# Queries and keys turned unsplit, two fp32 transposes in place of four fp32r ones, and split into high and low parts after the turn

## The chip, the cores and the metric

One core of a Trainium2 chip runs the whole program in one launch. The metric is device time in microseconds (us) of one execution. Engines are named as in the profile: PE is TensorE, DVE is VectorE, ACT is ScalarE, POOL is GpSimd, SP is the queue that issues most DMAs.

## What is computed

Two layers of a gated block over 528 tokens (16 meta tokens and 512 others) of width 1024. Each layer projects the normalised rows with one wide weight, and from the projection come attention queries (8 heads of 64), one key and one value head, index queries (8 heads of 64), one index key, a pooled branch and gates. The index scores choose 128 keys for each query, and attention runs over those.

```python
def hybrid_layer(x, norm_g, w_in, qn_g, kn_g, ...):
    h = rms_norm(x, norm_g)
    proj = jnp.einsum('btd,de->bte', h, w_in)
    q, k, v, gate_a, u_b, gate_b, q_idx, k_idx, w_idx, merge = jnp.split(proj, ...)
    q = apply_rope(rms_norm(q.reshape(B, T, 8, 64), qn_g), cos_h, sin_h)
    k = apply_rope(rms_norm(k, kn_g), cos, sin)
    q_idx = apply_rope(q_idx.reshape(B, T, 8, 64), cos_h, sin_h)
    k_idx = apply_rope(k_idx, cos, sin)
    attn = indexer_sparse_attention(q, k, v, q_idx, k_idx, w_idx, k_top)
    ...
# in the attention, for a block of queries
s = jnp.einsum('bqhd,bkd->bqhk', q_idx, k_idx)
score = jnp.einsum('bqhk,bqh->bqk', jax.nn.relu(s), w_idx * idx_scale)
_, sel = lax.top_k(score, k_top)
logits = jnp.einsum('bqhd,bqkd->bqhk', q, k[sel]) * attn_scale
```

## The kernel before, in words

**Precision by parts.** Most products run in fp32r, a shortened form of fp32. To keep accuracy, an operand is split into a high part (the value rounded to fp32r by an ACT copy) and a low part (the value less its high part, a DVE subtraction). A dense product is then three matmuls: high by high, low by high, high by low. A head of 64 numbers has room for both of its parts side by side: 64 partitions of high and 64 of low make one operand of 128 partitions. The key operand holds its high part in both halves (`KK[:, 0]`) and its low part in both halves (`KK[:, 1]`), so two matmuls give all four products of a head. `KI` is the same for the index key.

**Tokens and tiles.** `TOK` (line 26) cuts the tokens into a tile of 16 (t = 0, the meta tokens) and four of 128. Queries and keys come out of PE with tokens on the partitions, and have to be turned, so that the 64 numbers of a head lie on the partitions.

**What happens to a key tile** (`kv_post`, line 604). DVE multiplies the key (`g` = 0) and the index key (`g` = 1) by the rotation tables into `t1` and `t2`, POOL adds the two (line 633). In `second` DVE scales the key by its inverse norm, and ACT writes the high part twice into `ks` (line 640). In `third` DVE writes the low part twice. In `trans` PE turns the four blocks of `ks`, 128x128 fp32r each, and ACT copies the turned blocks into `KK` and `KI` (lines 650 and 651).

**What happens to a query tile** (`q_post`, line 656). A tile holds four heads. DVE makes `t1` and `t2`, POOL adds them (line 677), `second` writes the high parts into `qs` (ACT, line 686), `third` the low parts (DVE), `trans` turns four blocks of 128x128 fp32r (high and low of a head beside each other) and ACT copies 128x512 numbers into `qi` (index queries) or `qq` (queries) at line 697. There are 16 tiles of index queries and 16 of queries over both layers, 8 key tiles of 128 tokens and 2 of 16. The queries of the 16 meta tokens go through `q_post` with t = 0.

**What sets the order.** PE and DVE run in the order of the program text. ACT, POOL and SP are ordered by a scheduler. The text is paced by groups: `group_done` (line 367) ends a group of some 24 matmuls, and runs what `later(fn, n)` put off by n groups, then one piece of weight preparation, then pieces of the top-k selection (`sel`) as far as a budget of modelled PE and DVE times allows. `half_done` (line 361) is called twice in a group and issues index products or attention steps from `fill`. An index query's products are put into `fill` six groups after its projection (`FI`). PSUM tiles of turned blocks come from the ring `bank("a")`, four banks.

**Weights.** Each chunk of 256 columns is split as well. Some have their low part from ACT and a POOL DMA, others from DVE: the weight chunk of the second half of the index queries is split by two DVE subtractions of 128x1024 early in each layer, and the first matmuls that read its low part stand in the first group of that chunk, 16 matmuls after the group's begin.

**PE's transposes** name the turned tile and the unit matrix as operands: `a<-identr,qs` and `a<-identr,ks` are the fp32r ones, `a<-consts,lt` are transposes of unsplit fp32 tiles in the attention (line 821), where `consts` holds the fp32 unit matrix.

Of the kernel before, what the change touches and what calls it, by code (L numbers as in the profile page):

```python
# [91 lines left out]
def tile_block(ctx: ExitStack, tc: tile.TileContext, x, meta, w_in, pool_w, w_a, w_b, w_out, rows, hgain, c_tab, out):  # L92
# [10 lines left out]
    def f(ap):  # L103
        return ap.bitcast(F32)
# [3 lines left out]
    def bank(tag, dt=F32):  # L108
        return psum.tile([128, 512], dt, tag=tag, name=tag, bufs=BANKS[tag])
# [246 lines left out]
    credit = [0.0]  # L356

# [3 lines left out]
    def half_done():  # L361
        credit[0] += rate[0] / 2
        n = int(credit[0])
        credit[0] -= n
        pump(n)
# [24 lines left out]
    def flush():  # L390
        while pend:
            pend.popleft()[1]()
# [211 lines left out]
    def kv_post(l, t, ps):  # L604
# [9 lines left out]
        v1 = t1[:m, :128].rearrange("p (g d) -> p g d", g=2)  # L614
        for g, (C, S) in enumerate(((Cg, Sg), (ctab, stab))):
            dve.tensor_tensor(v1[:, g], p2[:, g], C[:m, t], op=OP.mult)
            dve.tensor_tensor(t2[:m, 64 * g:64 * g + 64].rearrange("p (a d) -> p a d", a=2),
                              p2[:, g].rearrange("p (a d) -> p a d", a=2)[:, ::-1, :],
                              S[:m, t].rearrange("p (a d) -> p a d", a=2), op=OP.mult)
# [13 lines left out]
        gp.tensor_tensor(t1[:m, :128], t1[:m, :128], t2[:m, :128], op=OP.add)  # L633
        ks = tmp.tile([128, 4, 128], F32R, tag="P", name="ks", bufs=PB)
        k4 = ks[:m].rearrange("p (g a) (b d) -> p g a b d", g=2, b=2)
        b1 = v1[:, :, None, :].to_broadcast([m, 2, 2, 64])

        def second():
            dve.tensor_scalar(t1[:m, :64], t1[:m, :64], rk[:m], None, op0=OP.mult)
            act.copy(k4[:, :, 0], b1)  # L640

        def third():
            dve.tensor_sub(k4[:, :, 1], b1, f(k4[:, :, 0]))

        def trans():
            tp = bank("a", F32R)
            for j in range(4):
                pe.transpose(tp[:, j * 128:j * 128 + m], ks[:m, j, :], identr[:m, :m])
            t4 = f(tp).rearrange("p (g j c) -> p g j c", g=2, j=2)
            act.copy(KK[:, :, s:s + m], t4[:, 0, :, :m])  # L650
            act.copy(KI[0][:, :, s:s + m], t4[:, 1, :, :m])
        later(second, 1)
        later(third, 2)
        later(trans, 4)

    def q_post(t, ps, normed, dst, g=0):
# [21 lines left out]
        if normed:  # L678
            qs = tmp.tile([128, 544], F32R, tag="L", name="qs", bufs=LB)[:, :512].rearrange("p (h c) -> p h c", h=4)
        else:  # L680
            qs = tmp.tile([128, 4, 128], F32R, tag="P", name="qs", bufs=PB)

        def second():
            if normed and t == 0:
                dve.tensor_tensor(v1, v1, rq[:m, :, None].to_broadcast([m, 4, 64]), op=OP.mult)
            act.copy(qs[:m, :, 0:64], v1)
            if normed and t:
                norms()
# [10 lines left out]
        later(third, QN if normed else QI)  # L699
        later(trans, QN + 1 + l if normed else QI + 1)  # L700
# [3 lines left out]
    def index_steps(i, g, qS):  # L704
        n = NK[i]
        for hh in range(4):
            h = 4 * g + hh
            r = tmp.tile([128, 544], F32, tag="L", name="r", bufs=LB)
            for o, w in KPARTS[i]:
                ps = bank("a")  # L710
                pe.matmul(ps[:, :w], qS[:, hh, :], KI[0][:, 0, o:o + w], start=True, stop=False)
                pe.matmul(ps[:, :w], qS[:, hh, :], KI[0][:, 1, o:o + w], start=False, stop=True)
                e = min(w, n - o)
                act.activation(r[:, n - 1::-1] if i == 0 else r[:, o:o + e], ps[:, :e], AF.Relu,  # L714
                               scale=wab[:, i, h:h + 1])
# [41 lines left out]
    def attention(ensure, later_rate, on):  # L757
        st, pvs, pms, turned = {}, {}, {}, []

        def logits(u):  # L760
# [7 lines left out]
            for hh in range(2):  # L768
                h = 2 * j + hh
                qS = QS[i, h // 4][:, h % 4, :]  # L770
# [811 lines left out]
```

## Time and profile before

| | |
|---|---|
| median of 3 runs | 738.46 us (737.41 to 738.52) |
| span of the profiled execution | 735.6 us, 2.9 us below the median of the runs |
| PE busy | 730.1 us (99%), 5949 matmuls |
| DVE busy | 586.2 us (80%) |
| ACT busy | 482.1 us (66%) |
| POOL busy | 254.2 us (35%) |
| granted TensorE clock | 0.999 |

The span runs from the first to the last instruction of the program. A row of the groups names the line, engine, operation, tiles (out<-in), partitions and shape, then the busy time, the mean of one and the idle time before. Matmuls overlap one another, so the mean duration of one is longer than what it takes of PE's time. What it takes is read from the starts of rows in the timeline: the time from the start of one row to the start of the next.

### The profile page before, as it was taken

How to read it: one execution, taken by the hardware profiler on the slowest of the kernel's cores; microseconds unless marked ns; L12 is line 12 of the kernel's file. 1: busy time of each engine (PE TensorE's matmuls, PEld its weight loads, DVE VectorE, ACT ScalarE, POOL GpSimd, SP SyncE). 2: the span in 40 equal slices, each digit the busy share in tenths (PEclk: the TensorE clock that was granted, in tenths of full speed). 3: DMA queues.
4: the chain of work that ended last, by engine and by line, in shares of the span. 5: the costliest groups of instructions: out<-in, count | busy, mean ns of one | idle time of the engine just before them, and what ended most of it. 6: DMA issues, size and time to landing. Idle time of an engine off the chain costs nothing.

```text
span 735.6 us, 16083 instructions
## 1 busy us (share of the span) xinstructions
PE 730.1 (99%) x5949; PEld 706.0 (96%) x5949; DVE 586.2 (80%) x1478; ACT 482.1 (66%) x1099; POOL 254.2 (35%) x336
## 2 busy tenths in 40 slices
PE   9999999999999999999999999999999999999998
PEld 8999998999999999999999989998899999999997
DVE  6966999998997775894348668999989978768874
ACT  6779735757788886543245796357588977775643
POOL 3751174731222211163247411757131231106300
PEclk9999999999999999999999999999999999999999
DMA  8767765964655434643523778659564654438832
GB/s 268 233 172 165 167 145 115 229 149 99 141 119 122 94 84 105 192 141 118 143 89 87 171 175 199 157 116 205 126 156 103 144 115 90 113 107 268 202 88 71
DMA packets 103566, 106.41 MB, mean 145 GB/s; under 512 B 5008, under 2 KB 83632, under 8 KB 103488
## 3 DMA queue, kind: packets, MB, share of 16 engines
q1 hardware_dynamic: 91888, 74.89, 34.5%
q0 software_dynamic: 11520, 30.41, 23.1%
q8 instruction: 46, 0.75, 0.4%
q14 instruction: 32, 0.26, 0.1%
q10 hardware_dynamic: 80, 0.08, 0.0%
HBM read 66.41 MB, written 8.55 MB: 102 GB/s over the span
## 4 chain that ended last, share of the span: by engine, by line
PE 99%; DVE 0%; issue 0%; ACT 0%; DVEq 0%
PE d L63 80%; PE a L63 13%; PE v L63 5%; DVE ot L63 0%; DVE w L63 0%; ACT w L269 0%; ACT osum L1121 0%; DVE idle L63 0%; DVE nf L63 0%; DVE ta L63 0%; DVEq L63 0%; DVE ones L63 0%; ACT p L1021 0%; DVE ss L63 0%; DVE mhalf L63 0%
## 5 line engine op out<-in xcount | busy, mean ns | idle before, releaser
L63 PE MATMUL d<-hhi,w 128*128 128x256 f32 (+3 forms) x1392 | 278.4, 291 | 0.0
L63 PEld LDWEIGHTS d<-hhi,w 128*128 128x128 f32 x1392 | 222.2, 188 | 3.0 <-issue 0.6
L63 PE MATMUL d<-hlo,w 128*128 128x256 f32 (+3 forms) x696 | 189.8, 289 | 0.0
L63 DVE TENSOR_TENSOR w<-raw,w 128x512 fp32r<-128x512 f32 (+1 forms) x156 | 121.5, 785 | 14.0 <-ACT w L269 13.2
L63 PEld LDWEIGHTS d<-hlo,w 128*128 128x128 f32 x696 | 131.3, 189 | 1.4 <-issue 0.2
L63 PE MATMUL d<-hsum,w 128*128 128x264 f32 (+1 forms) x720 | 95.5, 285 | 0.0
L63 PEld LDWEIGHTS d<-hsum,w 128*128 128x128 f32 x720 | 89.6, 188 | 0.7 <-issue 0.3
L63 PE MATMUL d<-w,hhi 128*128 128x256 f32 x576 | 86.1, 287 | 0.0
L269 ACT CAST w<-raw 128x512 fp32r<-128x512 f32 x132 | 79.0, 624 | 6.7 <-DMA raw<-s 5.9
L63 PEld LDWEIGHTS d<-w,hhi 128*128 128x128 f32 x576 | 74.7, 188 | 4.7 <-issue 3.5
L255 POOL DMA_DIRECT2D raw<-raw x22 | 19.9, 905 | 115.5 <-DMA raw<-in_w_in_dram 30.3
L63 DVE MATCH_REPLACE8 sc<-m,sc 128x400 f32<-128x400 f32 (+2 forms) x100 | 54.4, 547 | 0.0
L221 POOL DMA_DIRECT2D w<-raw x34 | 31.8, 951 | 64.1 <-ACT w L220 46.5
L63 DVE MAX8 m<-sc 128x8 f32<-128x400 f32 (+2 forms) x100 | 53.2, 556 | 0.9
L793 ACT ACTIVATE lt<-lt,mn,NR 128x144 f32<-128x144 f32 (+3 forms) x64 | 42.3, 663 | 12.8 <-DVE mn L63 12.8
L284 POOL DMA_DIRECT2D raw<-s x22 | 19.6, 891 | 87.9 <-DVE s L63 40.7
L63 DVE SCALAR_TENSOR_TENSOR sc<-r,wsg,sc 128x144 f32<-128x144 f32 (+3 forms) x56 | 32.4, 582 | 16.9 <-ACT r L714 14.7
L63 PE MATMUL d<-w,hlo 128*128 128x256 f32 x288 | 45.6, 281 | 0.0
L63 PE MATMUL d<-mhi,w 128*128 128x272 f32 (+2 forms) x192 | 45.5, 324 | 0.0
L808 POOL TENSOR_SCALAR pm<-lt,rs 128x16 f32<-128x16 f32 x48 | 26.3, 575 | 44.2 <-DVE rs L63 33.1
L677 POOL TENSOR_TENSOR t<-t,t 128x256 f32<-128x256 f32 (+1 forms) x34 | 32.3, 951 | 25.6 <-DVE t L63 25.2
L1427 POOL TENSOR_TENSOR hlo<-ta,hhi 128x256 fp32r<-128x256 f32 (+1 forms) x28 | 26.8, 965 | 41.6 <-PE d L63 29.4
(247 smaller groups left out, 1564.5 us busy)
## 6 DMA issues: line engine op xcount, KB each, us to landing
raw<-in_w_in_dram SPq DMA_DIRECT2D x88, 256.0 KB, 3.5
w<-raw POOLq DMA_DIRECT2D x34, 512.0 KB, 5.9
raw<-in_w_in_dram SPq DMA_DIRECT2D x32, 512.0 KB, 4.6
raw<-in_w_out_dram SPq DMA_DIRECT2D x12, 512.0 KB, 3.8
raw<-raw POOLq DMA_DIRECT2D x22, 256.0 KB, 4.2
raw<-s POOLq DMA_DIRECT2D x22, 256.0 KB, 3.7
kept<-res SPq DMA_DIRECT2D x16, 264.0 KB, 3.2
res<-kept SPq DMA_DIRECT2D x16, 264.0 KB, 6.2
```

The costliest lines, as they stand in the source:

```text
L63: return fn(*a, **k)
L221: gp.dma_start(t, raws[c][s], accum_op=OP.add)
L255: gp.dma_start(raws[c][0][:, 1], raws[c][0][:, 0], accum_op=OP.add)
L269: act.copy(t[:, 0], blk[src[n]])
L284: gp.dma_start(blk["a12"], blk["s2"], accum_op=OP.add)
L677: added[0] = gp.tensor_tensor(t1[:m, :256], t1[:m, :256], t2[:m, :256], op=OP.add).ins
L793: act.activation(L[hh][:, :n], L[hh][:, :n], AF.Exp, scale=NR[:, i, h:h + 1], bias=mn[:, hh:hh + 1], accum_out=sm[:, hh:hh + 1])
L808: (gp if j < 3 else dve).tensor_scalar(pms[i][:, 2 * j + hh, :], L[hh][:, 0:16], rs[:, hh:hh + 1], None, op0=OP.mult)
L1427: pool_end = gp.tensor_sub(hlo[:, j, a:a + n], d, f(hhi[:, j, a:a + n]))
```

## The change

- Unsplit fp32 tiles are turned. A query tile has two transposes of 128x128 fp32, each of two heads side by side, in place of four of fp32r. A key tile has two, one for the key and one for the index key, each of which lies twice beside itself, so that both halves of the partitions get it. For that the POOL sum writes 256 numbers per row (128 before), and DVE's scaling 128 (64 before).
- The parts are made after the turn. A turned block has one head on partitions 0 to 63 and another on 64 to 127, and the parts of a head have to end on both halves. For index queries ACT copies the turned block into `qf` in SBUF and writes each head's high part in its own half, and DVE subtracts into the other half (two subtractions of 64x256). For queries ACT writes the high parts of both heads of a block, DVE subtracts out of PSUM into the low parts (128x256), and one group later two ACT copies of 64x256 move a low part and a high part to the other half (`cross`). For keys ACT copies the turned block into `kf`, writes two high parts, and DVE subtracts twice.
- The heads of a tile then lie in another order, and `place(h)` gives the place of a head.
- A new queue, `soon`, holds DVE's subtractions until the second `half_done` after the transposes.
- An index query's transposes come one group earlier than before (there are no parts to wait for), those of a meta key tile one group earlier, those of the others in the same group as before. The meta tokens' queries are as before.

The diff, cut to its core:

```diff
     def half_done():
+        ticks[0] += 1
+        while soon_q and soon_q[0][0] <= ticks[0]:
+            soon_q.popleft()[1]()
         credit[0] += rate[0] / 2
...
+    def soon(fn):
+        soon_q.append((ticks[0] + 2, fn))
...
-        gp.tensor_tensor(t1[:m, :128], t1[:m, :128], t2[:m, :128], op=OP.add)
-        ks = tmp.tile([128, 4, 128], F32R, tag="P", name="ks", bufs=PB)
...
+        gp.tensor_tensor(t1[:m, :256].rearrange("p (g b d) -> p g b d", g=2, b=2),
+                         *(v2[:, o, :, None, :].to_broadcast([m, 2, 2, 64]) for o in range(2)), op=OP.add)
         def second():
-            dve.tensor_scalar(t1[:m, :64], t1[:m, :64], rk[:m], None, op0=OP.mult)
-            act.copy(k4[:, :, 0], b1)
-
-        def third():
-            dve.tensor_sub(k4[:, :, 1], b1, f(k4[:, :, 0]))
+            dve.tensor_scalar(t1[:m, :128], t1[:m, :128], rk[:m], None, op0=OP.mult)
 
         def trans():
-            tp = bank("a", F32R)
-            for j in range(4):
-                pe.transpose(tp[:, j * 128:j * 128 + m], ks[:m, j, :], identr[:m, :m])
-            t4 = f(tp).rearrange("p (g j c) -> p g j c", g=2, j=2)
-            act.copy(KK[:, :, s:s + m], t4[:, 0, :, :m])
-            act.copy(KI[0][:, :, s:s + m], t4[:, 1, :, :m])
+            tp = bank("a")
+            kf = tmp.tile([128, HB], F32, tag="tt", name="kf", bufs=6)
+            for g in range(2):
+                pe.transpose(tp[:, g * m:g * m + m], t1[:m, g * 128:g * 128 + 128], ident[:m, :m])
+            act.copy(kf[:, :2 * m], tp[:, :2 * m])
+            sides = [(K[:, 0, s:s + m], K[:, 1, s:s + m], kf[:, g * m:g * m + m]) for g, K in enumerate((KK, KI[0]))]
+            for hi, lo, k in sides:
+                act.copy(hi, k)
+
+            def low():
+                for hi, lo, k in sides:
+                    dve.tensor_sub(lo, k, f(hi))
+            soon(low)
         later(second, 1)
-        later(third, 2)
-        later(trans, 4)
+        later(trans, 4 if t else 3)
...
+        def paired():
+            tp = bank("a")
+            for b in range(2):
+                pe.transpose(tp[:, b * 128:(b + 1) * 128], t1[:, b * 128:(b + 1) * 128], ident)
+            own, other = slice(0, 64), slice(64, 128)
+            both = tp[:, :256].rearrange("p (b c) -> p b c", b=2)
+            if normed:
+                act.copy(dst[:, 0:2], both)
+
+                def cross():
+                    act.copy(dst[other, 0:2], f(dst[own, 2:4]))
+                    act.copy(dst[own, 2:4], both[other])
+                soon(lambda: dve.tensor_sub(dst[:, 2:4], both, f(dst[:, 0:2])))
+                later(cross, 1)
+                return
+            qf = tmp.tile([128, HB], F32, tag="tt", name="qf", bufs=6)[:, :256].rearrange("p (b c) -> p b c", b=2)
+            act.copy(qf, both)
+            heads = [(dst[own, 0:2], dst[other, 0:2], qf[own]), (dst[other, 2:4], dst[own, 2:4], qf[other])]
+            for hi, lo, q in heads:
+                act.copy(hi, q)
+
+            def low():
+                for hi, lo, q in heads:
+                    dve.tensor_sub(lo, q, f(hi))
+            soon(low)
+
+        if t:
+            if normed:
+                later(norms, 1)
+            later(paired, QN + 1 + l if normed else QI)
+            return
...
-        later(third, QN if normed else QI)
-        later(trans, QN + 1 + l if normed else QI + 1)
+        later(third, QN)
+        later(trans, QN + 1 + l)
+
+    def place(h):
+        return 2 * (h % 2) + h % 4 // 2
```

How the order moves on PE, in the first layer, from the end of the fourth key tile's projection on. Before (`ks` are the split keys, `qs` the split index queries, `VM` the meta values):

```order
L63 MATMUL a<-identr,ks 128x128 x8
L63 MATMUL a<-VM,consts 128x64
L63 MATMUL d<-w,hhi 128x256 x8
L63 MATMUL d<-w,hlo 128x256 x8
L63 MATMUL d<-w,hhi 128x256 x8
L63 MATMUL a<-identr,ks 128x16 x4
L63 MATMUL a<-identr,qs 128x128 x4
```

The same place of PE's order after the change (`t_292` and `t_308` are the key tiles 1 and 2, `t_407` the meta key tile, `t_415` and `t_447` the index queries of tiles 1 and 2):

```order
L63 MATMUL a<-consts,t_292 128x128 x2
L63 MATMUL a<-consts,t_308 128x128 x2
L63 MATMUL a<-VM,consts 128x64
L63 MATMUL a<-consts,t_407 128x16 x2
L63 MATMUL a<-consts,t_415 128x128 x2
L63 MATMUL d<-w,hhi 128x256 x8
L63 MATMUL d<-w,hlo 128x256 x8
L63 MATMUL d<-w,hhi 128x256 x8
L63 MATMUL a<-consts,t_447 128x128 x2
```

The eight transposes of two key tiles are four, the meta key and the first index query have moved ahead of a group of 24 matmuls, and the dense matmuls stand as they did.

DVE's order at the same point of the second layer, from the low part of the second index query to the second half of the weight chunk. Before (`t_5767` is key tile 4, `w<-raw,w` a half of the low part of the weights):

```order
L63 TENSOR_TENSOR qs<-t_5691,qs 128x4x64
L63 TENSOR_TENSOR ks<-t_5714,ks 128x2x128
L63 TENSOR_SCALAR t_5767<-t_5767,rk 128x64
L63 TENSOR_TENSOR t_5829<-d,consts 128x256
L63 TENSOR_TENSOR t_5830<-d,consts 128x256
L63 TENSOR_TENSOR w<-raw,w 128x1024
L63 TENSOR_TENSOR ks<-t_5767,ks 128x2x128
L63 TENSOR_TENSOR t_5871<-d,consts 128x256
L63 TENSOR_TENSOR t_5872<-d,consts 128x256
L63 TENSOR_TENSOR w<-raw,w 128x1024
```

DVE's order there after the change (`t_5744` is key tile 4; three subtractions of 128x128 into `KK` and `KI` stand ahead of the first row):

```order
L63 TENSOR_TENSOR KI<-kf,KI 128x128
L63 TENSOR_TENSOR KK<-kf,KK 128x16
L63 TENSOR_TENSOR KI<-kf,KI 128x16
L63 TENSOR_TENSOR qi<-qf,qi 64x256 x2
L63 TENSOR_SCALAR t_5744<-t_5744,rk 128x128
L63 TENSOR_TENSOR t_5804<-d,consts 128x256
L63 TENSOR_TENSOR t_5805<-d,consts 128x256
L63 TENSOR_TENSOR w<-raw,w 128x1024
L63 TENSOR_TENSOR qi<-qf,qi 64x256 x2
L63 TENSOR_TENSOR t_5839<-d,consts 128x256
L63 TENSOR_TENSOR t_5840<-d,consts 128x256
L63 TENSOR_TENSOR w<-raw,w 128x1024
```

The subtractions into `ks` and `qs` ahead of the transposes are gone, and subtractions into `KK`, `KI` and `qi`, which wait for PE's transposes and ACT's copies of them, stand ahead of both halves of the weights.

More of the change, by code (lines that the diff above doesn't have):

```diff
@@ L356, in tile_block @@
     credit = [0.0]
+    soon_q, ticks = deque(), [0]
+    def soon(fn):
+        soon_q.append((ticks[0] + 2, fn))
     sel = deque()
@@ L390, in flush @@
     def flush():
-        while pend:
-            pend.popleft()[1]()
+        while pend or soon_q:
+            (soon_q if soon_q else pend).popleft()[1]()
     def drain():
@@ L613, in kv_post @@
         t2 = tmp.tile([128, HB], F32, tag="tt", name="t2", bufs=6)
-        v1 = t1[:m, :128].rearrange("p (g d) -> p g d", g=2)
+        v2 = t2[:m, :256].rearrange("p (o g d) -> p o g d", o=2, g=2)
         for g, (C, S) in enumerate(((Cg, Sg), (ctab, stab))):
-            dve.tensor_tensor(v1[:, g], p2[:, g], C[:m, t], op=OP.mult)
-            dve.tensor_tensor(t2[:m, 64 * g:64 * g + 64].rearrange("p (a d) -> p a d", a=2),
+            dve.tensor_tensor(v2[:, 0, g], p2[:, g], C[:m, t], op=OP.mult)
+            dve.tensor_tensor(v2[:, 1, g].rearrange("p (a d) -> p a d", a=2),
                               p2[:, g].rearrange("p (a d) -> p a d", a=2)[:, ::-1, :],
@@ L677, in q_post @@
         added[0] = gp.tensor_tensor(t1[:m, :256], t1[:m, :256], t2[:m, :256], op=OP.add).ins
[L678 to L681, printed above, removed]
+        def paired():
[26 more added lines that the diff above has]
+            return
+        qs = tmp.tile([128, 544], F32R, tag="L", name="qs", bufs=LB)[:, :512].rearrange("p (h c) -> p h c", h=4)
         def second():
-            if normed and t == 0:
-                dve.tensor_tensor(v1, v1, rq[:m, :, None].to_broadcast([m, 4, 64]), op=OP.mult)
+            dve.tensor_tensor(v1, v1, rq[:m, :, None].to_broadcast([m, 4, 64]), op=OP.mult)
             act.copy(qs[:m, :, 0:64], v1)
-            if normed and t:
-                norms()
         def third():
@@ L710, in index_steps @@
                 ps = bank("a")
-                pe.matmul(ps[:, :w], qS[:, hh, :], KI[0][:, 0, o:o + w], start=True, stop=False)
-                pe.matmul(ps[:, :w], qS[:, hh, :], KI[0][:, 1, o:o + w], start=False, stop=True)
+                pe.matmul(ps[:, :w], qS[:, place(hh), :], KI[0][:, 0, o:o + w], start=True, stop=False)
+                pe.matmul(ps[:, :w], qS[:, place(hh), :], KI[0][:, 1, o:o + w], start=False, stop=True)
                 e = min(w, n - o)
@@ L769, in logits @@
                 h = 2 * j + hh
-                qS = QS[i, h // 4][:, h % 4, :]
+                qS = QS[i, h // 4][:, place(h), :]
                 for pi, (o, w) in enumerate(KPARTS[i]):
```

2 lines of the change are left out of this document (removed).

## The prediction

> **What bounds the kernel now.** I read the page first: the busy times, the chain that ended last and the granted clock.
>
> ```profile
> span 735.6 us, 16083 instructions
> PE 730.1 (99%) x5949; PEld 706.0 (96%) x5949; DVE 586.2 (80%) x1478; ACT 482.1 (66%) x1099; POOL 254.2 (35%) x336
> ...
> PEclk9999999999999999999999999999999999999999
> ...
> PE 99%; DVE 0%; issue 0%; ACT 0%; DVEq 0%
> ```
>
> PE is busy for 99% of the span at full clock, and 99% of the chain that ended last is PE itself. So what is taken off PE's stream shortens the program, and what is added to ACT, DVE or POOL costs nothing unless PE comes to wait for it. Next I asked what PE waits for. The list of waits has one entry for it:
>
> ```profile
> PE d L63 <- DVE ss L63: 1.5, 1, 1.5
> ```
>
> That one lies in the start, before any query. So there is no stall in the stages of the change that could hide a gain, and none whose going would add to it. A busy PE is not PE at its best, so the next question is what the transposes take of PE's time.
>
> **What the old transposes take.** The groups of PE, by shape, give the counts: index queries and queries, and keys.
>
> ```profile
> L63 PE MATMUL a<-identr,qs 128*128 128x128 f32 x128 | 14.9, 240 | 0.0
> L63 PE MATMUL a<-identr,ks 128*128 128x128 f32 x32 | 3.8, 252 | 0.0
> L63 PE MATMUL a<-consts,lt 128*128 128x128 f32 x160 | 22.7, 272 | 0.0
> ```
>
> 128 fp32r transposes are 32 query tiles of four, 32 are 8 key tiles of four. The third row is the nearest to the new ones: fp32 tiles turned with the fp32 unit matrix. The means are durations of overlapping matmuls and not what each takes, so I take that from starts. One whole group of PE's timeline in the first layer, from one turn of a query tile to the next:
>
> ```profile
> 50.32 0.46 PE L63 MATMUL a<-identr,qs 128*128 128x128 f32 x4
> 50.61 1.18 PE L63 MATMUL d<-w,hhi 128*128 128x256 f32 x8
> 51.63 1.11 PE L63 MATMUL d<-w,hlo 128*128 128x256 f32 x8
> 52.58 1.11 PE L63 MATMUL d<-w,hhi 128*128 128x256 f32 x8
> 53.52 0.45 PE L63 MATMUL a<-identr,qs 128*128 128x128 f32 x4
> ```
>
> From 50.32 to 53.52 are 3.20 us. Eight dense matmuls take 52.58 - 51.63 = 0.95, so 24 take 2.85, and the four transposes 0.35, each 0.088. The same for two fp32 transposes in the attention, with 12 dense matmuls between them and the last row:
>
> ```profile
> 180.88 0.38 PE L63 MATMUL a<-consts,lt 128*128 128x128 f32 x2
> 181.02 0.37 PE L63 MATMUL d<-hhi,w 128*128 128x264 f32 x1
> 181.22 0.28 PE L63 MATMUL d<-hlo,w 128*128 128x264 f32 x1
> ...
> 182.56 0.65 PE L63 MATMUL d<-hsum,w 128*128 128x264 f32 x4
> ```
>
> From 181.22 to 182.56 run 11 dense matmuls in 1.34, each 0.122. From 180.88 to 182.56 are 1.68, less 12 x 0.122 = 1.46: two fp32 transposes take 0.22, each 0.11. An fp32 transpose costs a quarter more than an fp32r one, and there are half as many.
>
> **PE's sum.** A query or key tile of 128 tokens goes from 0.35 to 0.22: 0.13 less. There are 40 such tiles (32 + 8): 5.2 us. The two meta key tiles have transposes of 16 tokens:
>
> ```profile
> 35.13 0.48 PE L63 MATMUL a<-identr,ks 16*128 16x16 f32 x4
> 35.54 0.54 PE L63 MATMUL a<-identr,qs 128*128 128x128 f32 x4
> ```
>
> Four take 0.41, so two some 0.2 if each costs the same, 0.4 over both layers. Together 5.6 us off PE. The end of the range: rows of two decimals leave 0.02 in each tile, so 4.8 to 6.4.
>
> The Trainium skill, in "FP8 and Floating Point Precision", section TensorE Precision Notes, says that true fp32 makes four passes through the array. By that a turn in fp32 would be dearer and not cheaper; what it would make of the sum is a rival below. The trace does not bear it out for transposes: 0.11 against 0.088 is no factor of four.
>
> **ACT, DVE and POOL.** These lie beside PE, so I count what they gain or lose and then ask who is late. Rows for the prices:
>
> ```profile
> L686 ACT CAST qs<-t 128x256 fp32r<-128x256 f32 x32 | 13.1, 408 | 16.9 <-POOL t L677 16.8
> L697 ACT CAST qq<-a 128x512 fp32r<-128x512 f32 x16 | 9.5, 592 | 1.6 <-PE a L63 1.6
> L823 ACT COPY pt<-a 128x256 f32<-128x256 f32 x16 | 5.9, 371 | 0.4 <-PE a L63 0.4
> L225 ACT CAST w<-raw 128x1024 fp32r<-128x1024 f32 x34 | 35.3, 1056 | 0.0
> L63 DVE TENSOR_TENSOR qs<-t,qs 128x256 fp32r<-128x256 f32 x32 | 16.1, 503 | 0.0
> L633 POOL TENSOR_TENSOR t<-t,t 128x128 f32<-128x128 f32 x8 | 3.8, 484 | 0.1
> L677 POOL TENSOR_TENSOR t<-t,t 128x256 f32<-128x256 f32 x32 | 30.9, 965 | 20.0 <-DVE t L63 19.6 <-PE d L63 0.3
> ```
>
> - A query tile on ACT: before 0.41 + 0.59 = 1.00. After, an index tile has 0.37 (out of PSUM) and two copies of 64x256, which I take at the 0.41 of 128x256, since a row has as many numbers: 1.19. A query tile has 0.37 + 0.41 + 0.37 = 1.15. Over 32 tiles ACT gains some 5.5 us of work.
> - On DVE an index tile goes from one subtraction at 0.50 to two, 0.5 more, 8 us over 16 tiles; a query tile keeps one. The subtractions of 64x256 that write the other half are not in the trace. From below they cost the same as 128x256 (a row has as many numbers), from above I allow twice that; I take the same.
> - POOL's sum for a key tile grows by 0.97 - 0.48 = 0.5, 5 us over ten.
>
> The stretches of the index stage in both layers show the room for it (columns: PE, PEld, DVE, ACT, POOL):
>
> ```profile
> 45.00:75.00 30.00, 30.00 (x252) 30.00 (x252) 18.82 (x41) 25.46 (x53) 6.67 (x8) 1.00 0.74 172
> 412.00:440.00 28.00, 27.97 (x186) 25.24 (x185) 17.48 (x39) 23.94 (x50) 6.84 (x9) 1.00 0.80 182
> ```
>
> DVE has 11 us free in each, and takes on 4. ACT, at 85%, is the narrow one, and takes on some 1.5. Neither becomes the bound there; what can go wrong is order, not load.
>
> **Who is late.** DVE's subtractions used to stand ahead of PE's transposes; now they stand behind them and wait for PE, then for two or three ACT copies. Behind a waiting subtraction stand all later DVE instructions. In the index stage these are the next tile's rotations and, at the start of each layer, the low parts of a weight chunk. For an index tile the text leaves half a group to a whole one from the transposes to the subtraction, and one more to the first product. A group is 3.2 us, and the chain of three copies (1.2) and two subtractions (1.0) is 2.2. So the products find their operand ready if neither queue is more than 2 us behind. The tightest place that I find is the weight chunk, whose low parts come in two halves. The second layer before, first DVE, then PE:
>
> ```profile
> 404.29 0.26 DVE L63 TENSOR_SCALAR t<-t,rk 128x64 f32<-128x64 f32 x1 [0.35 <-POOL t L633]
> 404.46 0.75 DVE L63 TENSOR_TENSOR t<-d,consts 128x256 f32<-128x256 f32 x2
> 405.12 1.22 DVE L63 TENSOR_TENSOR w<-raw,w 128x1024 fp32r<-128x1024 f32 x1
> 406.25 0.95 DVE L63 TENSOR_TENSOR ks<-t,ks 128x256 fp32r<-128x256 f32 x1
> 407.13 0.74 DVE L63 TENSOR_TENSOR t<-d,consts 128x256 f32<-128x256 f32 x2
> 407.80 1.21 DVE L63 TENSOR_TENSOR w<-raw,w 128x1024 fp32r<-128x1024 f32 x1
> ```
>
> ```profile
> 408.95 1.10 PE L63 MATMUL d<-w,hhi 128*128 128x256 f32 x8
> ```
>
> The second half is done at 409.0. PE's row reads it from its fifth matmul on, at 409.4, so 0.4 us are to spare. By then the new PE is 0.7 early: 4 x 0.13 for two key and two index tiles, 0.2 for the meta tile. It needs the half at 408.7. DVE loses the subtraction of 406.25 (0.9 to the next start) and gets the two of the second index tile there. From below these take 0.66, as the two rotations from 404.46 to 405.12 do; from above 1.0. The scaling of 404.29 waits for a POOL sum that is up to 0.5 longer. So the half is done between 409.0 - 0.9 + 0.66 = 408.8 and 409.0 - 0.9 + 1.0 + 0.5 = 409.6, and PE waits 0.1 to 0.9. I take 0.5. The first layer has more room:
>
> ```profile
> 39.54 1.22 DVE L63 TENSOR_TENSOR w<-raw,w 128x1024 fp32r<-128x1024 f32 x1
> ```
>
> ```profile
> 41.75 1.10 PE L63 MATMUL d<-w,hhi 128*128 128x256 f32 x8
> ```
>
> The half is done at 40.8 and read from 42.2 on. With PE 0.7 early and DVE 0.5 late, 0.2 are left: no wait. All other places I take at nothing, covered by that one group; uncovered, an index tile costs up to the 2.2 us chain. New waits: 0.5.
>
> In the query stages the subtraction reads PSUM and ACT's `cross` reads the same bank a group later, so a bank of the ring is held for one to two groups. There are four banks and one turn in a group: no wait. The queries themselves are read only in the attention, many groups later.
>
> **The sum.** 735.6 - 5.6 + 0.5 = 730.5 of span. The median of the runs is 738.46, 2.9 above the span, which the change doesn't touch: 733.4 us, 0.7% less. A measurement of this kernel can tell a change of some 0.2%, 1.5 us, from none.
>
> **The rivals.**
> - Late halves, partly (chance 0.10). PE waits a little in each of 24 places, 16 index tiles and 8 key tiles. At 0.1 each it is 2.4 more: 735.8, still faster. For it: ACT at 85%. Against: the spare group.
> - Late halves, throughout (0.06). ACT's weight casts stand ahead of the copies, DVE stands behind ACT, and PE waits in each of the 16 index tiles. It decides at 5.6 / 16 = 0.35 us a tile; at 0.5 it is 8.0 - 5.6 = 2.4 over 738.5: 740.9. For it: ACT waits in order, and a weight cast takes 1.06 us. Against: DVE has 11 us free in the stage.
> - The time is taken back elsewhere (0.05): weights or gates arrive at their own pace and PE waits for them, 738.5. Against it: the one wait in the list.
> - fp32 in four passes (0.02). A pass over 128 columns takes half of a dense matmul of 256, 0.119 / 2 = 0.06; four take 0.24, two transposes 0.48 against 0.35 now. Over 40 tiles that is 5.2 more: 743.7. This is what the page's rule would do here, and the 160 transposes of `lt` speak against it.
>
> **The numbers.** My forecast has 0.77. The range reaches from 731.9 (6.4 off, no new wait, and 0.2 for the runs' spread) to 737.0, which takes in the first rival with the least gain, 4.8 (736.6), and 0.4 of spread; left out are the other three, 0.13. Faster by over 0.2%: 0.77 + 0.10 = 0.87. Within 0.2%: 0.05. Slower: 0.06 + 0.02 = 0.08.
>
> **What would show it.** Right: PE busy falls by about 5.6 with 84 matmuls fewer, the list of PE's waits stays as short, and from the start of a pair of the new transposes to the dense rows behind it takes 0.22 as with `lt`. Wrong: PE waiting for `qi`, `KI` or `w` between 30 and 75 or 395 and 440; a pair at 0.35 or more; PE stopped for more than 0.9 ahead of the fifth `d<-w,hhi` at that place. If PE's busy time falls as said and the span doesn't, the third rival holds.

## The result, and the profile after the change

| | before | after |
|---|---|---|
| median of the runs | 737.93 us (4 runs beside after) | 747.97 us (746.60 to 749.70) |
| ratio | | 1.0138, 95% interval 1.0117 to 1.0159 |
| span of the profiled execution | 735.6 us | 744.8 us |
| granted TensorE clock | 0.999 | 0.993 |

The change made the kernel 1.4% slower, where 0.7% faster was forecast. From the page after the change, the busy times and, as its last line here, the chain that ended last:

```profile
PE 728.6 (98%) x5865; PEld 703.4 (94%) x5865; DVE 602.4 (81%) x1504; ACT 489.0 (66%) x1131; POOL 256.0 (34%) x336
...
PE 81%; DVE 12%; ACT 3%; DMA 2%; issue 1%; SPq 1%; POOL 1%; DVEq 0%; ACTq 0%
```

The 84 matmuls are gone, but PE's busy time fell by 1.5 us only (730.1 to 728.6), and the chain that was 99% PE is 81% PE, and DVE has 12% of it. The list of PE's waits, one entry before, has seven:

```profile
PE a L63 <- ACT qi L703: 2.9, 1, 2.9
PE d L63 <- ACT sq L674: 2.2, 2, 1.7
PE a L63 <- POOL rk L502: 1.8, 1, 1.8
PE a L63 <- DVE qi L63: 1.8, 1, 1.8
PE d L63 <- DVE ss L63: 1.5, 1, 1.5
PE d L63 <- DVE w L63: 1.1, 1, 1.1
PE a L63 <- ACT kf L650: 0.9, 1, 0.9
```

Without the old one (ss, 1.5) that is 10.7 us of new waits. The transposes themselves cost what was forecast. One pair in the middle of the index stage (PE's timeline):

```profile
57.15 0.38 PE L63 MATMUL a<-consts,t 128*128 128x128 f32 x2
57.29 1.19 PE L63 MATMUL d<-w,hhi 128*128 128x256 f32 x8
58.32 1.10 PE L63 MATMUL d<-w,hlo 128*128 128x256 f32 x8
```

From 57.15 to 58.32 are 1.17, less eight dense matmuls at 0.119, 0.95: the pair takes 0.22. So the loss is all in waiting and in what follows it. The first of the places is the end of the first layer's key stage (PE's timeline; in brackets the idle time before the row and what ended it):

```profile
31.88 0.24 PE L63 MATMUL a<-consts,t 16*128 16x16 f32 x2
33.95 0.59 PE L63 MATMUL a<-consts,t 128*128 128x128 f32 x2 [1.82 <-POOL rk L502]
34.19 2.05 PE L63 MATMUL d<-w,hhi 128*128 128x256 f32 x8
36.04 1.75 PE L63 MATMUL d<-w,hlo 128*128 128x256 f32 x8
...
38.58 0.38 PE L63 MATMUL a<-consts,t 128*128 128x128 f32 x2
...
44.68 0.68 PE L63 MATMUL a<-KI,qi 128*128 128x144 f32 x2 [2.89 <-ACT qi L703]
```

At 33.95 PE turns the first index query into a fifth `a` bank in a row. (The row names POOL's `rk`; in the run rings below, the same wait is put down to ACT's copy into `kf`, which reads such a bank.) At 44.68 the first index product has waited for its low part. What DVE and ACT did meanwhile, DVE first:

```profile
34.64 0.28 DVE L63 TENSOR_SCALAR t<-t,rk 128x128 f32<-128x128 f32 x1
39.47 0.22 DVE L63 TENSOR_TENSOR t<-v,Cg 128x64 f32<-128x64 f32 x1 [4.55 <-ACT sq L616]
...
41.13 0.96 DVE L63 TENSOR_TENSOR KK<-kf,KK 128x128 fp32r<-128x128 f32 x1
...
42.89 0.28 DVE L63 TENSOR_TENSOR KK<-kf,KK 128x128 fp32r<-128x128 f32 x1
...
44.11 0.87 DVE L63 TENSOR_TENSOR qi<-qf,qi 64x256 fp32r<-64x256 f32 x2
```

```profile
35.31 0.85 ACT L703 CAST qi<-qf 64x256 fp32r<-64x256 f32 x2
39.00 0.22 ACT L616 ACTIVATE sq<-v 128x64 f32<-128x64 f32 x1 [2.83 <-PE a L63]
```

DVE stands idle for 4.55 us. It waits for ACT's `sq` of key tile 4, which is idle for 2.83 us itself and waits for PE. It isn't data that `sq` waits for: it reads the projection in `v`, which PE had finished by 31.24, before it turned the meta key at 31.88. PE's next row after the long group, at 38.58, turns the second index query out of its `t1`, and `sq` starts right behind it: my reading was that `sq` wants a buffer of the ring `tt`, and that the next one in turn is that `t1`. No view names the buffer; the run rings tests the reading. Behind DVE's waiting rotation stand the low parts of `KK`, `KI` and `qi`; of those of 128x128 one took 0.28 and another 0.96. Over the program that wait is the fourth on DVE's list (it isn't there before):

```profile
DVE t L63 <- ACT sq L616: 10.4, 5, 4.6
```

PE also ran slower after it had stood. Stretches of 3 us (columns: PE, PEld, DVE, ACT, POOL, then the granted clock, the DMA share and GB/s):

```profile
33.00:36.00 3.00, 2.05 (x10) 2.08 (x11) 1.92 (x11) 2.76 (x15) 1.17 (x2) 0.67 0.53 164
...
45.00:48.00 3.00, 3.00 (x17) 3.00 (x17) 2.93 (x5) 2.30 (x4) 1.89 (x2) 0.55 0.00 0
```

Eight dense matmuls took 36.04 - 34.19 = 1.85 us in place of 0.95. The starts of the dense matmuls, compared one by one with those of before, show that after falls behind by some 16 us in all and wins some 6.5 back: the steps are at 32 to 34, 39 to 40, 145, 399, 406 to 410 and 511 us of the old timeline, and between them the new kernel gains slowly, as forecast.

### The profile page after: what moved, and what is told of

Its sections match the earlier page's. It is cut to its first block, busy times and chain, and to the rows that moved or that the text cites. A ratio compares the mean times of both kernels' runs of the same rounds, so it can differ in the third digit from the quotient of the medians.

```text
span 744.8 us, 15963 instructions
## 1 busy us (share of the span) xinstructions
PE 728.6 (98%) x5865; PEld 703.4 (94%) x5865; DVE 602.4 (81%) x1504; ACT 489.0 (66%) x1131; POOL 256.0 (34%) x336
## 4 chain that ended last, share of the span: by engine, by line
PE 81%; DVE 12%; ACT 3%; DMA 2%; issue 1%; SPq 1%; POOL 1%; DVEq 0%; ACTq 0%
PE d L63 66%; PE a L63 10%; PE v L63 4%; DVE sc L63 2%; DVE t L63 2%; DVE m L63 2%; DMA xt<-in_x_dram 2%; DVE nf L63 1%; DVE w L63 1%; DVE hlo L63 1%; DMA raw<-in_w_in_dram 0%; DVE silb L63 0%; ACT w L220 0%; DVE mlo L63 0%; SPq L156 0%
## 5 line engine op out<-in xcount | busy, mean ns | idle before, releaser
L63 PE MATMUL d<-w,hhi 128*128 128x256 f32 x576 | 88.3, 292 | 1.1 <-DVE w L63 1.1
L63 PEld LDWEIGHTS d<-w,hhi 128*128 128x128 f32 x576 | 76.9, 193 | 5.9 <-issue 2.7
L63 PE MATMUL d<-w,hlo 128*128 128x256 f32 x288 | 47.2, 289 | 0.0
L842 POOL TENSOR_SCALAR pm<-lt,rs 128x16 f32<-128x16 f32 x48 | 27.8, 606 | 44.3 <-DVE rs L63 31.7
L63 PEld LDWEIGHTS d<-w,hlo 128*128 128x128 f32 x288 | 40.5, 196 | 0.0
L748 ACT ACTIVATE r<-a,wab 128x272 f32<-128x272 f32 (+2 forms) x80 | 35.4, 488 | 7.5 <-PE a L63 7.3
```

Of the source, the lines that this page charges most:

```text
L63: return fn(*a, **k)
L842: (gp if j < 3 else dve).tensor_scalar(pms[i][:, 2 * j + hh, :], L[hh][:, 0:16], rs[:, hh:hh + 1], None, op0=OP.mult)
```

## The experiments

Theory at the start: the ring `tt`. The change puts `kf` and `qf` into it and leaves `t1` there until PE has turned it, and so chains ACT, DVE and POOL to PE. Rivals: the low parts stand behind the turn in the queues' order; five banks in a row; the new operations are dear in themselves. Four repairs, put in one after another, took the time from 747.97 to 734.30. The runs of the kernel before beside them had medians of 737.5 to 738.1.

### The ring

**rings.** `t1` is moved to rings with room; `kf` and `qf` stay in `tt`.

```diff
-t1 = tmp.tile([128, HB], F32, tag="tt", name="t1", bufs=6)      # kv_post
+t1 = tmp.tile([128, HB], F32, tag="L", name="t1", bufs=LB)
-t1 = tmp.tile([128, HB], F32, tag="tt", name="t1", bufs=6)      # q_post
+t1 = tmp.tile([128, HB], F32, tag="L" if normed else "P", name="t1", bufs=LB if normed else PB)
```

> The changed kernel with one edit: t1, which now lives until PE has turned it, is taken out of the ring tt of six buffers (a key's t1 into the ring L, an index query's into P, a query's into L). sq, t2, kf and qf stay in tt. What is computed is the same, and the order of PE and DVE is the same. The ring theory (a tile takes three or four of the six tt buffers, so a buffer comes round after two tiles, and a t1 held for three or four groups makes ACT, DVE and POOL wait for PE's turn of a tile two earlier): the stalls of 3.05, 1.92 and 1.38 us go and so does most of the slow clock behind them; of the stalls of 1.93 and 0.96 for the fifth a bank in a row up to all may stay, with 1.85 uncertain; 734 to 738 us. The order theory (low parts stand behind the turn in ACT's and DVE's order, and that is what makes PE wait): nothing of the order is changed, 746 to 749 us. The bank theory (five a banks in a row): the stalls at 32 and 405 us stay, 745 to 748 us. Dear operations (fp32 turns, copies across halves): 746 to 749 us.

Measured: 741.88 us (741.02 to 742.51), ratio 1.0055 (1.004 to 1.007). 6.1 us came back with no instruction of PE or DVE moved, so order and dear operations don't explain those. Of ACT's order, which a scheduler makes, some 30 of 1131 instructions changed place. DVE's wait for `sq` shrank from 10.4 to 2.8 us. The `sq` of key tile 4 stands behind the same cast as in after, but here it starts without idle time, ahead of PE's turn of the second index query (at 35.92), so it had waited for a buffer and not for the turn's result:

```profile
35.07 0.22 ACT L616 ACTIVATE sq<-v 128x64 f32<-128x64 f32 x1
```

But 741.88 is above the range of the ring theory. The largest of the kernel's remaining waits:

```profile
PE d L63 <- DVE w L63: 2.4, 1, 2.4
PE a L63 <- DVE qi L63: 2.2, 2, 1.6
...
PE d L63 <- ACT zb L1420: 1.1, 1, 1.1
```

**old_ring4** was to be the control on the kernel before: its ring `tt` cut from six buffers to four and nothing else, 742 to 755 us by the ring theory. With four buffers its instructions wait for one another in a circle, so it gives no time, and no run shows the ring's waits without the change.

### Places in the order

**later.** The turns of index queries and meta keys go back by a group, with `t1` in `tt`. **rings_later.** The same with the rings moved.

```diff
-        later(trans, 4 if t else 3)
+        later(trans, 4)
-            later(paired, QN + 1 + l if normed else QI)
+            later(paired, QN + 1 + l if normed else QI + 1)
```

> The changed kernel with one edit: the turns of index queries and of the meta key tile are put back by one group, to where they stood before the change; t1 stays in the ring tt. The bank theory (five a banks in a row are wanted where the index query's turn comes directly behind the key tiles' and the meta values): the stalls at 32 and 405 us go with the slow clock behind them, 742 to 745 us. The ring theory: t1 is held a group longer, so the waits for a tt buffer grow, 748 to 753 us. The order theory: the low parts come a group later and the first products with them, so no gain, 747 to 751 us.

> Both edits: t1 out of the ring tt, and the turns of index queries and of the meta key tile a group later, as before the change. Ring and bank theory together: all six stalls go, and what is left is the gain of 5.6 us on PE, 732 to 734 us. Ring theory alone: as with the rings alone, 734 to 738 us. Order theory: 746 us or more.

Measured: 748.89 us (1.0146, 1.0131 to 1.0161) and 744.31 us (1.0085, 1.0068 to 1.0101), 2.4 more than rings. The first lies in the ranges of the ring and the order theory and outside that of the bank theory; for the second the expectation of 732 to 734 was a miss. The waits for a bank went in both, but the group that the turn lost was the one the products needed. The list of later:

```profile
PE a L63 <- DVE qi L63: 8.5, 2, 4.7
```

**rings_fi7.** From rings, `FI = 7`: the products come a group later.

> From the kernel rings one number: FI from 6 to 7, so that an index query's products come seven groups after its projection. Order theory, in the form that the spare group of the old order is all that the products lacked: the two waits for qi (1.64 and 0.54) go, the wait for w (2.45) stays since it stands in DVE's order and not in the products: 739 to 740 us. DVE and POOL theory: same. If the products were not what mattered: 741.9 us as in rings.

Measured: 744.42 us (1.0096, 1.0071 to 1.012), a miss. The waits for `qi` went, and PE came sooner to the next thing that DVE had not finished, the low weights, and waited 5.6 us there in four places:

```profile
PE d L63 <- DVE w L63: 5.6, 4, 2.5
```

So DVE itself was late at the start of a layer, and moving its readers only changed which of them waits.

### DVE beside POOL

What DVE did in rings, DVE first and then POOL, second layer:

```profile
403.72 0.28 DVE L63 TENSOR_TENSOR KK<-kf,KK 128x128 fp32r<-128x128 f32 x1
403.92 0.28 DVE L63 TENSOR_TENSOR KI<-kf,KI 128x128 fp32r<-128x128 f32 x1
404.12 0.98 DVE L63 TENSOR_TENSOR KK<-kf,KK 128x128 fp32r<-128x128 f32 x1
405.03 0.96 DVE L63 TENSOR_TENSOR KI<-kf,KI 128x128 fp32r<-128x128 f32 x1
```

```profile
404.07 0.89 POOL L493 TENSOR_TENSOR Cg<-consts,gains 128x320 f32<-128x320 f32 x1
404.91 0.93 POOL L494 TENSOR_TENSOR Sg<-consts,gains 128x320 f32<-128x320 f32 x1
```

The same subtraction takes 0.28 until POOL's tables begin at 404.07, and 0.98 and 0.96 beside them.

**psum.** From rings, without `kf` and `qf`: ACT and DVE read the turned bank, and DVE has one operand in SBUF, not two.

```diff
-            act.copy(kf[:, :2 * m], tp[:, :2 * m])
-            sides = [(K[:, 0, s:s + m], K[:, 1, s:s + m], kf[:, g * m:g * m + m]) for g, K in ...]
+            sides = [(K[:, 0, s:s + m], K[:, 1, s:s + m], tp[:, g * m:g * m + m]) for g, K in ...]
-            act.copy(qf, both)
-            heads = [(dst[own, 0:2], dst[other, 0:2], qf[own]), (dst[other, 2:4], dst[own, 2:4], qf[other])]
+            heads = [(dst[own, 0:2], dst[other, 0:2], both[own]), (dst[other, 2:4], dst[own, 2:4], both[other])]
```

> From the kernel rings (t1 out of the ring tt, 741.9 us) one edit: kf and qf are left out. ACT makes the high parts of keys and index queries straight out of the turned PSUM bank, and DVE subtracts out of that bank, so that its subtraction has one operand in SBUF and not two. In rings the six key subtractions took 0.28 us where POOL was idle and 0.70 to 0.98 where POOL's tables (L493, L494) ran, and an index pair 1.30 in place of 0.87. Theory that DVE and POOL hold each other up where DVE has two SBUF operands: the subtractions go back to about 0.3 each, DVE is through 2 to 2.5 us earlier, the waits for qi (1.64) and for w (2.45, with about 1.5 of slow clock behind it) shrink by 4 to 5: 736 to 738.5 us. Order theory (the low parts wait in line behind the turn and ACT, however long each takes): the waits stay, 741 to 743 us. Bank theory (a bank of the ring a is now held until DVE has subtracted): the wait for the fifth bank grows from 0.9 to 2 or 3, 742 us or more.

Measured: 739.85 us (1.0031, 1.0018 to 1.0045), 2.0 less, which lies in none of the three ranges. PE's wait for `w` is gone and that for `qi` fell from 2.2 to 0.2, as the theory of DVE beside POOL had it; its wait for a bank grew from 0.9 to 3.5, as the bank theory had it. The groups of DVE, first of rings, then of psum:

```profile
L63 DVE TENSOR_TENSOR qi<-qf,qi 64x256 fp32r<-64x256 f32 x32 | 15.2, 476 | 4.4 <-ACT qi L703 3.6
...
L63 DVE TENSOR_TENSOR KK<-kf,KK 128x128 fp32r<-128x128 f32 x8 | 5.1, 641 | 0.5 <-ACT KK L653 0.3
```

```profile
L63 DVE TENSOR_TENSOR qi<-a,qi 64x256 fp32r<-64x256 f32 x32 | 13.5, 422 | 2.9 <-ACT qi L699 2.3
...
L63 DVE TENSOR_TENSOR KK<-a,KK 128x128 fp32r<-128x128 f32 x8 | 2.3, 282 | 1.0 <-ACT KI L651 1.0
```

From 476 to 422 ns, and from 641 to 282. It isn't that they moved away from POOL. At the same place of psum, DVE first and then POOL, they lie beside the same tables:

```profile
404.56 0.28 DVE L63 TENSOR_TENSOR KK<-a,KK 128x128 fp32r<-128x128 f32 x1
404.75 0.28 DVE L63 TENSOR_TENSOR KI<-a,KI 128x128 fp32r<-128x128 f32 x1
```

```profile
403.93 0.87 POOL L493 TENSOR_TENSOR Cg<-consts,gains 128x320 f32<-128x320 f32 x1 [1.50 <-DVE t L63]
404.76 0.87 POOL L494 TENSOR_TENSOR Sg<-consts,gains 128x320 f32<-128x320 f32 x1
```

The Trainium skill, "SBUF — State Buffer", section Who interferes with whom, says that a DVE instruction with two inputs in SBUF contends with a GpSimd instruction that reads SBUF, and one with a single SBUF input doesn't. The rows agree. The edit also takes ACT's copies into `kf` and `qf` away, some 9 us of ACT's time over the program, and the run doesn't divide the 2.0 us between the two. The bank theory's part is the row of the fifth bank, in psum. It names `BV`: DVE's products read the bank of the meta values until 33.90, and the banks of the keys now wait for DVE's subtractions, which come later still:

```profile
34.05 0.41 PE L63 MATMUL a<-consts,t 128*128 128x128 f32 x2 [1.77 <-DVE BV L63]
```

### Five banks in a row

**psum_meta4** and **rings_meta4** put the meta key's turn alone back by a group (`later(trans, 4)`), from psum and from rings. **psum_vm4** puts the product of the meta values back instead (`later(meta_values, 4)` for 3), from psum. **psum_later_fi7** has both moves of the order above, from psum.

> From the kernel psum (739.85 us) one edit: only the turn of the meta key tile goes back one group, to where it stood before the change, so that four banks of the ring a are taken in a row and not five. Bank theory: the two waits of PE for a bank at 32 and 402 us (3.5 us in the list of waits, released by DVE's BV products) go, and with them about 3 us of slow clock behind them: 734 to 736 us. If the run of five is not the cause (for instance because the meta key's bank was the one held): the wait stays, 738.5 us or more.

> From the kernel rings (741.9 us) only the meta key's turn back by one group; kf and qf stay in SBUF. Bank theory: the wait of 1.0 at 33 us goes; the waits for qi at 40.7 us (1.8) and for w at 413 us (2.6, with 1.7 of slow clock) belong to DVE beside POOL and stay: 740 to 741.5 us. If all of it hung on the bank: 737 us or less.

> From the kernel psum (739.85 us) one edit: the product of the meta values (VM, which fills BV) goes back by one group, in place of the meta key's turn in psum_meta4. Again four banks of the ring a are taken in a row, and the meta key's low part stays early. Bank theory: the waits for a bank at 32 and 402 us (3.5 in the list, 3 of slow clock) go, and the waits for KI that psum_meta4 had (1.8) don't come: 734.5 to 736 us. If the meta key's own place was what helped: 738.5 us or more.

> The edits together: t1 out of the ring tt, no kf and qf, the turns of index queries and of the meta key tile a group later (as before the change), and the products a group later (FI 7). If the ring, the run of five banks, DVE beside POOL and the missing group are all that the change cost in the key and index stage, PE waits nowhere between 30 and 75 or 395 and 440 us, and only the waits of the query stage (1.1 and 0.9) are left: 733 to 735 us. If something else costs there: 737 us or more.

Measured: psum_meta4 737.18 us (0.9999, 0.999 to 1.0009), rings_meta4 742.28 (1.0063, 1.0048 to 1.0079), psum_vm4 736.36 (0.9978, 0.9966 to 0.999), psum_later_fi7 737.61 (0.9998, 0.9987 to 1.001). Two different ways of having four banks in a row end the waits of 1.8 and 1.7 at 32 and 402 us, so it was the run and not the meta key. psum_vm4 is 0.4 above its range: PE still waits 0.6 for a bank there, at 35.09. psum_meta4 misses its 734 to 736: it waits 1.8 us for DVE's `KI` (`PE a <- DVE KI`), 1.1 of it with products that need the meta key's low part, which now comes a group later, and 0.7 with a turn, which reads no `KI` and so waits for a bank. With the parts in SBUF the move brings nothing (rings_meta4, 0.8 above its range, 4.9 us of waits for `KI`); my reading is that DVE is later still there. psum_later_fi7 misses its 733 to 735 with waits of 1.8 us for ACT's `r`, whose place moved with the products.

### The query stage

**queries_only** has the queries as after the change (with `t1` in `L`), keys and index queries as before. **queries_direct** gives it two high parts by ACT and two subtractions of 64x256 by DVE, without copies across.

```diff
-            if normed:
-                act.copy(dst[:, 0:2], both)
-                ...
-                soon(lambda: dve.tensor_sub(dst[:, 2:4], both, f(dst[:, 0:2])))
-                later(cross, 1)
-                return
+            heads = [(dst[own, 0:2], dst[other, 0:2], both[own]), (dst[other, 2:4], dst[own, 2:4], both[other])]
```

> Only the queries as after the change (two fp32 turns of the unsplit tile, parts made behind, ACT copies across the halves; t1 in the ring L); keys and index queries as before it. On PE 16 tiles by 0.13 are 2.1 us less. Theory that the two waits of the query stage (1.1 to 1.9 at 145 us and 0.9 to 1.4 at 515 us) belong to the queries' own longer ACT work and its wait for DVE: 735.8 + 2 to 3, 737 to 738.5 us, no gain. Theory that they come only from the key and index stage running late: 735.5 to 736 us.

> From the kernel queries_only (737.5 us, no faster than before, with waits of 1.27 and 0.99 us in the query stage) one edit: the queries' parts go to their halves without ACT's two copies across. ACT writes two high parts of 64x256 out of PSUM, DVE subtracts twice 64x256 into the other half. ACT has 0.82 us a tile in place of 1.15 and no copy that waits for DVE; DVE has 0.88 in place of 0.42. Theory that ACT's copies across, in line ahead of sq and zb and themselves waiting for DVE, make the waits: both go, 735 to 736 us. Theory that DVE is late there (it has top-k work without a pause): the waits stay or grow, 737.5 to 739 us.

Measured: 737.54 us (0.9996, 0.9986 to 1.0006), in the range of the first theory, and 744.87 us (1.0099, 1.0082 to 1.0116), above both ranges. The queries alone gain nothing, and ACT's copies across are not the whole of it: without them PE still waits 1.1 for `zb`, and with 0.44 more on DVE a tile, 7.0 us over 16 tiles, the kernel is 7.3 us slower. What DVE gets there comes out in the time almost one for one. The stretches of queries_only, and then the stage in the kernel before:

```profile
125.00:135.00 10.00, 10.00 (x93) 9.10 (x92) 9.93 (x24) 6.95 (x14) 6.81 (x8) 1.00 0.45 113
135.00:145.00 10.00, 9.14 (x73) 8.30 (x71) 9.25 (x30) 6.87 (x16) 6.75 (x9) 1.00 0.89 223
145.00:155.00 10.00, 9.68 (x79) 9.46 (x80) 9.93 (x28) 7.33 (x17) 5.59 (x8) 1.00 1.02 230
```

```profile
127.00:156.00 29.00, 29.00 (x253) 27.54 (x252) 28.23 (x81) 21.38 (x47) 18.52 (x22) 1.00 0.93 217
```

DVE is busy for 29.1 of 30 us, ACT for 21.2. DVE was as full before, 28.23 of 29, with PE busy throughout. The text lets the top-k selection fill DVE to 1.05 of PE's modelled time, so my reading is that nothing is left for PE to be early with: what it gains it waits. A rival stays: in queries_only ACT works without a pause from 140.97 until the `zb` that PE waits for, started at 144.80, with two weight casts of 1.1 us in between, and no run takes ACT's line apart from DVE's there.

**queries_share** lowers that share in the query stage; **old_share** is the control.

```diff
         def queries(g):
             w = chunk()
+            share[0] = 0.95
```

> From the kernel queries_only (737.5 us) one number: in the query stage the top-k selection on DVE gets 0.95 of PE's modelled time and not 1.05. Theory that DVE sets the pace in the query stage (it works without a pause from 130 to 160 us in this kernel and is 1.1 us behind the kernel before at the fourth query's rotation), so that 2.1 us off PE turn into waits of 1.27 and 0.99: the waits go or shrink below 0.4, 735.5 to 736.5 us. Theory that ACT's copies across make the waits by themselves: they stay, 737.5 us.

> The kernel before with the same share of 0.95 in the query stage, as the control: it has no waits there, so 737.5 to 738.5 us, no difference. If it gains as well, what queries_share gains is not the change's.

Measured: 736.95 us (0.999, 0.9981 to 1.0) and 738.38 us (1.0007, 0.9994 to 1.0019). In queries_share the wait for `zb` (1.1) is gone and one of 0.9 is left. The time lies between the two ranges. The direction is that of the first theory and the control gains nothing, but 0.6 us is at the edge of what this measurement tells.

### All together

**psum_meta4_direct** has psum_meta4 and queries_direct's subtractions. **psum_vm4_share** has rings, parts out of PSUM, the meta values a group later and the share. **ring_back** is psum_vm4_share with `t1` back in `tt`.

> All four repairs on the changed kernel: t1 out of the ring tt, parts out of PSUM, the meta key's turn back by a group, queries without copies across. If the ring, DVE beside POOL, the run of five banks and the copies across are the whole loss, the forecast's gain of 5.6 us comes out: 732 to 734 us. If one of them is not a cause, 735 us or more, with its wait still in the list.

> The repairs of psum_vm4 and the share of 0.95 in the query stage together. If each removes its own waits, 732.5 to 734.5 us, the forecast of 733.4; if the selection that is put off comes to stand in the way of the attention, 736 us or more.

> The kernel psum_vm4_share (734.3 us, all repairs) with one of them undone: t1 is back in the ring tt of six, where it stays until PE has turned it. kf and qf are still left out, so a key tile takes three buffers and an index tile two. Ring theory: the key's sq and the queries' sq (ACT) and the rotations (DVE) wait again for PE's turn of a tile two before, and PE waits in the key stage and at 144 and 510 us: 737 to 742 us. If the ring was a cause only together with kf and qf, or not at all: 734 to 735 us.

Measured: psum_meta4_direct 745.10 us (1.0098, 1.0083 to 1.0113), a miss with the waits of queries_direct (3.2 for `w`, 3.0 for `sq`). psum_vm4_share 734.30 us (0.9957, 0.9944 to 0.9971), in its range and 0.4% faster than the kernel before. ring_back 735.22 us (0.9972, 0.9957 to 0.9987), far from the 737 to 742 of the ring theory and 0.2 above the other range. The two intervals overlap, so the 0.9 us between the two kernels isn't clear of noise. My ring theory was too wide in that. With `t1` back in `tt`, DVE's wait for `sq` is back in part (0.7 us in one place in psum_vm4_share, 4.0 in four in ring_back), but the time hardly shows it. So the 6.1 us come of `t1` and `kf`/`qf` in one ring together, three buffers for an index tile and four for a key tile. Moving `t1` out ends them, as rings shows; that leaving `kf` and `qf` out would do it too is what ring_back suggests, in a kernel that has the other repairs as well. The page of psum_vm4_share, and the longest of its waits:

```profile
PE 724.4 (99%) x5865; PEld 698.6 (95%) x5865; DVE 593.6 (81%) x1504; ACT 480.9 (66%) x1105; POOL 257.0 (35%) x336
```

```profile
PE d L63 <- DVE ss L63: 1.5, 1, 1.5
PE a L63 <- DVE KI L63: 0.9, 1, 0.9
```

## Why the prediction was wrong, point by point

| | us | less |
|---|---|---|
| after the change | 747.97 | |
| `t1` out of the ring (rings) | 741.88 | 6.1 |
| parts out of PSUM (psum) | 739.85 | 2.0 |
| four banks in a row (psum_vm4) | 736.36 | 3.5 |
| the selection's share (psum_vm4_share) | 734.30 | 2.1 |
| forecast | 733.4 | 0.9 |

These are steps of one path; the causes overlap, as ring_back shows, so another path would divide the 13.7 us in another way. A part of the 3.5 is the price of the step before it: PE's waits for a bank were 0.9 in rings and 3.5 in psum, where DVE too has to read a bank before it is free. The last step's two intervals overlap a little (0.9966 to 0.999 and 0.9944 to 0.9971).

- **PE's sum, 5.6 us: right.** A pair takes 0.22, and in psum_vm4_share PE is busy for 724.4, 5.7 less than before. After the change itself it was only 1.5 less, as the matmuls behind its stops took longer.
- **"All other places I take at nothing, covered by that one group": this step failed.** It counted the chain from a turn to its subtraction, 2.2 us, and took the queues on both sides as free. It didn't ask where `kf`, `qf` and the longer-lived `t1` lie. With a ring of six and three or four buffers a tile, the first instruction of a new tile waits for PE's turn of an earlier one, and DVE stood for 4.55 us in a place where the text had left a whole group.
- **"There are four banks and one turn in a group: no wait": failed at the start of a layer.** The order that stands in the part on the change has five tiles of `a` in a row (two keys, meta values, meta key, first query), and PE waited there for 1.8 and 0.9 us. It was said of the query stage only, and the count wasn't made where turns had moved together.
- **DVE's prices.** Two subtractions across the halves take 0.87 where POOL is idle, inside the 0.66 to 1.0 of the working. Beside POOL a pair took 1.30 (rings, at 409.73), which it had no term for. The trace of before could have told the rest, in three subtractions of one shape within 2 us:

```profile
400.98 0.42 DVE L63 TENSOR_TENSOR qs<-t,qs 128x256 fp32r<-128x256 f32 x1
...
402.00 0.92 DVE L63 TENSOR_TENSOR qs<-t,qs 128x256 fp32r<-128x256 f32 x1
402.84 1.09 DVE L63 TENSOR_TENSOR ks<-t,ks 128x256 fp32r<-128x256 f32 x1
```

  The two long ones lie beside POOL's tables, which run there from 401.77 to 403.65. I took them as the spread of a mean, and didn't ask which new ones would lie there.
- **The second layer's weight chunk, 0.1 to 0.9 of wait.** The place was right, the size wasn't: PE stood 1.1 there after the change, and 2.4 in rings. The working counted the index queries' subtractions and had no term for the key tiles' low parts, which stand ahead of that half of the weights in DVE's order: in rings six of them take from 403.72 to 406.70.
- **The query stage, taken at nothing.** The working asked for the tile's own path, and not what DVE has left, 0.8 of 29 us: queries_only has the 2.1 us less on PE and gains none of them.
- **The rival "late halves, throughout"** had the side right with 0.06. Its mechanism was wrong: PE waited for `qi` in two places (2.9 and 1.8), not in each of 16 tiles, and ACT's weight casts were not in the way there, ACT stood idle for 2.83 us ahead of 39.00. (In the query stage two casts from 147.74 to 149.74 do stand ahead of the `sq` that PE waits 1.7 for.) And it priced waits alone; of the 16 us lost the waits are 10.7, and some 5 are slow matmuls behind them, which no term held.

Left open: how the 6.1 us divide between a later `t1` and the two new tiles. Neither a longer ring `tt` nor the changed kernel with `kf` and `qf` alone left out was run.

## What to carry to other kernels

When an operand is to live longer, or a step gets a new buffer, count the buffers of its ring per tile and ask whose turn frees the next one: a ring that comes round too soon makes engines wait in line for an engine they don't depend on. Where PE is 99% busy, a wait on it costs its length, and here often the slow matmuls behind it: 10.7 us of waits and some 5 behind them outweighed 5.6 us of saved matmuls. A gain on PE may not show in a stage where another engine is filled to PE's time, so ask whether a budget that paces one engine by another has to be lowered with it.

## What the runs showed of the hardware

After a stop of PE the granted clock fell: to 0.55 from 45 to 48 us in after, behind a stop of 2.9 us. Behind the kernel's start, seven stops of 2.4 us or more stand in the runs: 2.89 in after, 2.45 in rings, 4.71 and 3.77 in later, 3.43 in rings_later, 2.50 in rings_fi7 and 2.87 in rings_meta4. Taking the starts of the matmuls in the 4.5 us behind each, against the usual distance from such a row to the next, they lost some 1.4 to 2.2 us (an estimate). Most single stops of 0.6 to 2.0 us were followed by a loss of 0.4 or less, as the one of 1.6 for `qi` in rings, which ended at 40.74. The stretch behind it has the clock at 1.00:

```profile
42.00:45.00 3.00, 3.00 (x28) 3.00 (x27) 2.91 (x6) 3.00 (x6) 2.69 (x2) 1.00 0.20 34
```

Length alone doesn't decide. Stops of 1.7 to 1.8 in the key stage, with only turns and narrow matmuls ahead of them, lost some 1.6 (at 34 us in after, with the clock at 0.67 above, and at 34 and 404 in psum), and one of 1.8 at 414.8 in after lost 1.3, while one of 2.0 in rings_meta4 lost 0.2. The Trainium skill, "TensorE: Matmul & The Clock Gate", section What's actually happening, puts the fall at an idle window of about 3.4 us that runs freely; here less was enough.
